# A hybrid encoder block: where attention's low value parts live, and when weights, sums and copies are begun beside it

## The chip, the cores and the metric

The kernel runs on one core of a Trainium2 chip. The metric is the device time of one execution in microseconds, as the median of several runs. PE stands for TensorE's matmul, PEld for its weight loads, DVE for VectorE, ACT for ScalarE, POOL for GpSimd and SP for SyncE, which issues most DMAs here.

## The reference

A stream of 16 learned meta tokens and 1024 tokens of width 1024 goes through one layer. u is the normed input, z = u @ w_in its projection into ten parts. Branch A is a bidirectional retention of four heads in chunks of 128, branch B a windowed attention of eight heads that share two groups of keys and values. The cut below leaves out the norms, gates and padding.

```python
def step(state, kv_c):
    return chunk_decay * state + kv_c, state
...
o_r = _bidirectional_retention(rq, rk, rv, lg_f, lg_b)   # forward scan + backward scan over chunks
y_r = (groupnorm(o_r) * ret_nw * silu(rg)) @ w_rb
...
s = concat(q . k over 3 neighbouring chunks, q . k over the meta keys) * scale
m = max(s, sink);  p = exp(s - m) / (sum(exp(s - m)) + exp(sink - m))
o_a = p @ v                                              # band and meta values
y_a = (o_a * silu(ag)) @ w_ab
mix = sigmoid(gr) * y_r + sigmoid(ga) * y_a
return h + rms_norm(mix @ w_out) * post_w
```

## The kernel before, in words

**Numbers in two parts.** An operand of a matmul is split into a high part (a cast to float32r) and a low part (the operand less its high part), and a product is three matmuls, high by high, low by high and high by low (`mm3`, line 71). So nearly everything that PE reads first passes one cast, on ACT or POOL, and one subtraction on DVE (`dve_lo`, line 88). A weight unit is 256 columns wide; it comes from HBM in two halves of 512 KB each (`fetch_w`, tag `wr`, two buffers) and `split_w` (line 108) makes `wh` on ACT or POOL and `wl` on DVE, both halves one after the other.

**Retention** (`retention`, line 451) runs for four heads. For each head a forward scan over nine chunks (`stage1`, `stage2`) is followed by a backward scan from chunk 8 to 1 (line 585): DVE advances the state `Sb`, POOL and DVE split it, PE forms `pb`, DVE adds it to `op`, takes the group's mean and variance, POOL the power of the variance, DVE normalises `op`, and two chunks later PE transposes it (`to`, line 574), ACT evacuates it to `ost` and SP stores pairs of chunks to `oTr_d`. A filler gives PE other matmuls in between: for heads 0 to 2 the next head's queries and keys, for head 3 the attention keys of group 0, parts of the gate products and the first attention query projection. The rotated queries and keys' sums live in tiles of pool `ra`: tag `q` has six buffers of 512 columns (`qr` of the retention heads, then `aq` of the attention queries, then the softmax rows `p` of even heads).

**Attention.** After retention its pool `rp` is closed and its memory is given to the pools `ap` and, from the other side, `aw` (line 1259). `gen_av` (line 1266) projects the values of the nine chunks: `pav` in one of three PSUM banks `pj`, then its high part `vah` on ACT and its low part `val` on DVE. `vah` lies in a pool that was there before; `val` (line 1263) lies in `ap`. Meta values go to `vm`. Then 32 chunks follow, four pairs of heads (hp) by eight blocks (n), counted here from 0 to 31. `stage1` (line 1287) makes the scores `ps` of both heads in the two PSUM banks `p2`, a masked maximum on DVE (line 1318) into `raw`, the exponential on ACT into `p`, a reciprocal on DVE and the scaling of `p` on POOL. `stage2` (line 1335) transposes `p` on PE into `pt1` and `pt2` (two banks, `p1`), and splits them: `pah` on ACT and `pal` on DVE, `pm` for the meta keys, `pbh` and `pbl` for the third key block. `stage3` (line 1369) multiplies with the values into `po`, ACT evacuates it to `oa` and SP stores it to `oTa_d`.

**The order of the work.** The loop at line 1398 puts, for each chunk k, stage 1 of chunk k+1, stage 2 of k, a number of fill steps (`FILL`, line 26) and stage 3 of k-1. A fill step is three matmuls. The fill is one list of projections (line 1389): attention queries `paq`, keys `pak` of group 1, and parts of the gate products `pe`. Beside it run the hooks (`BEGUN`, line 1425): after fill step n the functions listed under n are recorded. They fetch weights (`fetch_aq`, `fetch_ak`, `pre_fetch`, `sum_fetch`), split them (`parts_aq`, `parts_ak`, `pre_parts`), split queries (`split_q`, line 638: `aqh` on ACT, `aql` on DVE), split keys (`keys`, line 677: `kTh`, `kTl`), and form differences of x (`sum_row`, line 713). `hooked` (line 790) records them behind the last exponential and reciprocal (`marks`); `tc.issue_after` and `follow` tell the scheduler what to put them behind, and it then fixes one order for each engine. `x_to_out` (line 1438) copies 768 of the 1024 rows of x to the output in three DMAs on SP; it is recorded after chunk 13. After attention come the gate, branch and output products (`bz`, `br`, `ba`, `bo`), which are near half of the span.

## Time and profile before

| | |
|---|---|
| median of 3 runs | 1091.0 us (1089.63 to 1092.32) |
| the profiled execution | 1090.71 us |
| its span, first to last instruction | 1088.9 us |
| mean granted TensorE clock | 0.993 |
| ACT, POOL busy | 47%, 19% |
| DMA | 175.17 MB, 161 GB/s on the mean |

The span is what the trace shows; the execution's time has 1.8 us more around it. Retention ends near 340 us, attention runs from there to about 590 us, and the rest are the gate, branch and output products. Matmuls are pipelined: a row of PE lasts longer than the distance to the next one, so work is counted by the distance of rows and lost time by what a stretch took beyond that. A row's last bracket gives the idle time before it on its engine and what ended it.

### The profile page before, as it was taken

The page shows a single profiled execution, that of the slowest core. Times are in us where ns is not written, and L with a number is a line of the kernel's source. Part 1 is how long each engine was busy: PE and PEld are TensorE (multiplying, and loading weights), DVE is VectorE, ACT ScalarE, POOL GpSimd, SP SyncE. Part 2 cuts the span into 40 slices and gives each one's busy share as a digit, 9 for nine tenths or more (in the row PEclk, how much of TensorE's full clock was granted, in tenths as well). Part 3 has the DMA queues.
Part 4 walks back from the last instruction along what each step waited for, and adds up shares of the span by engine and source line. Part 5 has one row for each costly group of instructions (what it writes and reads, how often), then busy time and mean ns, then how long its engine had stood idle before and what let it go on. Part 6 is the DMA issues. An engine that isn't in the chain of part 4 may idle for free.

```text
span 1088.9 us, 17108 instructions
## 1 busy us (share of the span) xinstructions
PE 1060.2 (97%) x5939; PEld 914.8 (84%) x5939; DVE 878.6 (81%) x1789; ACT 510.1 (47%) x1118; POOL 209.8 (19%) x268
## 2 busy tenths in 40 slices
PE   8999999999998999998999999999999999999997
PEld 6898999988988888887888888887888888787886
DVE  7897778878975777877867999999889889867765
ACT  7241432512513556655567654545556546433442
POOL 3234225233332222322320000000000000010032
PEclk9999999999998999999999999999999999999999
DMA  7121102113121152452357678899944656779463
GB/s 289 39 69 58 47 34 69 58 49 98 50 78 39 45 173 94 155 194 88 126 170 263 245 259 286 268 363 331 376 175 139 221 201 199 230 203 324 137 116 78
DMA packets 82902, 175.17 MB, mean 161 GB/s; under 512 B 8784, under 2 KB 22608, under 8 KB 82000
## 3 DMA queue, kind: packets, MB, share of 16 engines
q1 hardware_dynamic: 78928, 167.51, 44.9%
q0 software_dynamic: 3456, 6.29, 3.7%
q8 instruction: 47, 0.77, 0.3%
q14 instruction: 39, 0.32, 0.1%
q10 hardware_dynamic: 432, 0.28, 0.1%
HBM read 119.52 MB, written 57.67 MB: 163 GB/s over the span
## 4 chain that ended last, share of the span: by engine, by line
PE 81%; DVE 9%; DMA 6%; issue 2%; ACT 2%; POOL 0%; SPq 0%; DVEq 0%; POOLq 0%; ACTq 0%
PE bz L73 6%; PE bz L74 6%; PE bz L75 6%; PE pv L73 3%; PE pv L74 2%; PE pv L75 2%; PE br L74 2%; PE br L75 2%; PE br L73 2%; PE bo L74 2%; PE bo L73 2%; PE bo L75 2%; PE ba L74 2%; PE paq L74 2%; PE ba L75 2%
## 5 line engine op out<-in xcount | busy, mean ns | idle before, releaser
L1180 POOL DMA_DIRECT2D mx_d<-c1a x4 | 3.7, 920 | 401.8 <-DVE c1a L1171 401.8
L75 PE MATMUL bz<-T,lhz 128*128 128x512 f32 x192 | 75.8, 395 | 0.0
L74 PE MATMUL bz<-T,llz 128*128 128x512 f32 x192 | 75.8, 395 | 0.0
L73 PE MATMUL bz<-T,lhz 128*128 128x512 f32 x192 | 75.2, 394 | 0.0
L73 PE MATMUL pv<-wh,big 128*128 128x256 f32 x256 | 73.1, 286 | 1.2 <-DVE m_qk L181 1.2
L74 PE MATMUL pv<-wh,big 128*128 128x256 f32 x256 | 73.0, 285 | 0.0
L75 PE MATMUL pv<-wl,big 128*128 128x256 f32 x256 | 72.7, 284 | 0.0
L74 PE MATMUL bz<-big,llz 128*128 128x512 f32 x176 | 69.7, 396 | 0.0
L73 PE MATMUL bz<-big,lhz 128*128 128x512 f32 x176 | 69.1, 396 | 0.4 <-ACT lhz L880 0.3
L75 PE MATMUL bz<-big,lhz 128*128 128x512 f32 x176 | 69.3, 394 | 0.0
L1321 ACT ACTIVATE p<-raw,nm 128x401 f32<-128x401 f32 (+1 forms) x64 | 38.3, 599 | 48.9 <-DVE nm L1318 48.9
L1331 POOL TENSOR_SCALAR p<-p,den 128x400 f32<-128x400 f32 (+1 forms) x60 | 38.7, 659 | 110.6 <-DVE den L1324 109.0
L73 PE MATMUL paq<-big,wh 128*128 128x512 f32 x128 | 51.8, 405 | 0.0
L74 PE MATMUL paq<-big,wl 128*128 128x512 f32 x128 | 50.6, 396 | 0.0
L75 PE MATMUL paq<-big,wh 128*128 128x512 f32 x128 | 50.4, 394 | 0.0
L73 PEld LDWEIGHTS pv<-wh,big 128*128 128x128 f32 x256 | 48.2, 188 | 1.7 <-DVE m_qk L181 1.5
L74 PEld LDWEIGHTS pv<-wh,big 128*128 128x128 f32 x256 | 48.2, 188 | 0.2
L75 PEld LDWEIGHTS pv<-wl,big 128*128 128x128 f32 x256 | 48.3, 189 | 0.0
L1318 DVE CUSTOM_DVE_ANT_0 raw<-ps,mask,nsink 128x400 f32<-128x400 f32 (+1 forms) x64 | 36.1, 597 | 13.8 <-PE ps L75 13.6
L75 PEld LDWEIGHTS bz<-T,lhz 128*128 128x128 f32 x192 | 36.2, 188 | 8.4
L73 PEld LDWEIGHTS bz<-T,lhz 128*128 128x128 f32 x192 | 36.2, 188 | 8.4
L74 PEld LDWEIGHTS bz<-T,llz 128*128 128x128 f32 x192 | 36.2, 188 | 8.4
(630 smaller groups left out, 3624.9 us busy)
## 6 DMA issues: line engine op xcount, KB each, us to landing
wrz<-in_w_in_dram SPq DMA_DIRECT2D x32, 512.0 KB, 5.7
wr<-in_w_in_dram SPq DMA_DIRECT2D x29, 512.0 KB, 3.6
e<-e SPq DMA_DIRECT2D x40, 256.0 KB, 3.7
we<-in_w_in_dram SPq DMA_DIRECT2D x16, 512.0 KB, 3.8
tg<-tg_d SPq DMA_DIRECT2D x32, 256.0 KB, 5.0
T<-preT SPq DMA_DIRECT2D x6, 1024.0 KB, 7.6
oTr_d<-ost SPq DMA_DIRECT2D x16, 256.0 KB, 2.1
xs<-in_xT_dram SPq DMA_DIRECT2D x8, 512.0 KB, 3.8
```

Source lines behind the costliest of these rows:

```text
L73: nc.tensor.matmul(o, ah, bh, start=first, stop=False, **kw)
L74: nc.tensor.matmul(o, al, bh, start=False, stop=False, **kw)
L75: latest[:] = [nc.tensor.matmul(o, ah, bl, start=False, stop=last, **kw).ins]
L1180: nc.gpsimd.dma_start(d, to, accum_op=ALU.add)
L1318: nc.vector.tensor_tensor_reduce(raw[e_][:, 1:1 + wid], s[:, 0:wid], mask[:, mo:mo + wid], -SCALE, nsink[:, hd:hd + 1], ALU.add, ALU.min, ...
L1321: last["exp"] = nc.scalar.activation(p[:, 0:1 + wid], raw[e_][:, 0:1 + wid], AF.Exp, scale=-1.0, bias=nm_[:, e_:e_ + 1], accum_out=den[:, ...
L1331: nc.gpsimd.tensor_scalar(pt[e_][:, 0:wid], pt[e_][:, 0:wid], den[:, e_:e_ + 1], 1.0, op0=ALU.mult, op1=ALU.mult)
```

## The change

Five things change. (1) `val` becomes four tiles of the ring `q` in pool `ra`, two chunks in each, in place of a tile of `ap`; the softmax rows `p` of both heads now come from `ap` with four buffers. (2) The order at the start of attention: the last two value chunks are recorded behind the last transposition of retention (`last["to"]`) and ahead of stage 1 of chunk 0, and chunk 0's fill goes before its stage 2. (3) A weight's two halves are split by two hooks some steps apart (`half_w`), the gate weights' sums are split from their parts (`pre_sums`, `pre_parts`), and `sum_row` comes in two parts; the last lo and hi operations of a chunk join the marks that hooks are recorded behind. (4) `FILL` gives the first two head pairs 114 steps (before 105) and the last two 86 (95), and `BEGUN` has new places for nearly all hooks. (5) `x_to_out` is recorded after chunk 17 in place of 13, and the list of fill has `gen_aq(2, 1)` and `gen_ak(1, (2, 3))` unbroken.

```diff
-FILL = (8, 8, 6, 7, 6, 6, 7, 6), (6, 7, 6, 6, 7, 6, 6, 7), (7, 8, 8, 6, 6, 6, 7, 7), (6, 6, 5, 5, 5, 5, 8)
+FILL = (8, 8, 7, 7, 7, 7, 7, 7), (7,) * 8, (7, 6, 6, 6, 6, 6, 6, 5), (5, 5, 5, 5, 5, 5, 8)
...
-    def split_w(raw, u, act=False):
+    def halves_w(u):
         hi, lo = [], []
-        for s, t in enumerate(raw):
-            h = wp.tile([P, 4, 256], R, tag="wh", bufs=4, name=f"wh{u}_{s}")
-            l = wp.tile([P, 4, 256], R, tag="wl", bufs=4, name=f"wl{u}_{s}")
+
+        def split(t, act):
+            h, l = (wp.tile([P, 4, 256], R, tag=f"w{x}", bufs=4, name=f"w{x}{u}_{len(hi)}") for x in "hl")
             if act:
                 nc.scalar.copy(h, t)
             else:
             dve_lo(l, t, h)
             hi.append(h)
             lo.append(l)
-        return (lambda k, a, b: hi[k // 4][:, k % 4, a:b]), (lambda k, a, b: lo[k // 4][:, k % 4, a:b])
+
+        return split, ((lambda k, a, b: hi[k // 4][:, k % 4, a:b]), (lambda k, a, b: lo[k // 4][:, k % 4, a:b]))
 
     def load_w(src, u, act=False):
-        return split_w(fetch_w(src, u), u, act)
+        split, w = halves_w(u)
+        for t in fetch_w(src, u):
+            split(t, act)
...
+                last["to"] = nc.tensor.transpose(to[:, P * e_:P * e_ + P], o[:, P * e_:P * e_ + P], ident).ins
...
-        wq[hp] = fetch_w(w_in, U_AQ + hp)
-
-    def parts_aq(hp):
-        wq[hp] = split_w(wq[hp], U_AQ + hp, True)
+        raw = fetch_w(w_in, U_AQ + hp)
+        split, wq[hp] = halves_w(U_AQ + hp)
+        begun["q", hp] = lambda s: split(raw[s], True)
+
+    def fetch_ak():
+        raw = fetch_w(w_in, U_AK)
+        split, w_ = halves_w(U_AK)
+        wak.append(w_)
+        begun["k", 1] = lambda s: split(raw[s], True)
+
+    def half_w(which, i, s):
+        begun[which, i](s)
+
+    begun = {}
...
-    def sum_row(k):
+    def sum_row(k, part):
 
         x = {}
         for i, t in xsum.items():
-            nc.scalar.activation(t, t, AF.Copy, scale=vec[:, 4 * i + k:4 * i + k + 1])
+            if not part:
+                nc.scalar.activation(t, t, AF.Copy, scale=vec[:, 4 * i + k:4 * i + k + 1])
             for j in range(2):
                 x[i, j] = t[:, 512 * j:512 * j + 512]
-        for n, o, a, b in SUMS:
+        for n, o, a, b in SUMS[2 * part:2 * part + 2]:
...
-    def pre_parts(u):
+    def pre_sums(u):
 
         g = nc.vector.tensor_tensor
-        raw, n = fetched_w.pop(u), P * len(PRE[u])
+        raw, n = fetched_w[u], P * len(PRE[u])
         t = raw[-1]
         if n > P:
             v = t[:, :, P:n]
             g(v, raw[0][:, :, P:n], v, ALU.add)
             g(v, v, raw[0][:, :, 0:P], ALU.subtract)
             g(v, t[:, :, 0:P], v, ALU.subtract)
+
+    def pre_parts(u):
+
+        t, n = fetched_w.pop(u)[-1], P * len(PRE[u])
...
-                with follow(*marks("exp", "sum")):
+                with follow(*marks("exp", "sum", "lo", "hi")):
...
+    val = [ra.tile([P, 512], R, tag="q", bufs=6, name=f"val{b}") for b in range(NB // 2)]
     pm = [ap.tile([P, 256], R, name=f"pm{i}") for i in range(2)]
-    val = ap.tile([P, NB, 256], R, name="val")
     for t in (vm, pm[0], pm[1]):
         nc.vector.memset(t.bitcast(F32), 0.0)
+    def low_value(b):
+        return val[b // 2][:, 256 * (b % 2):256 * (b % 2) + 256]
...
-                nc.vector.scalar_tensor_tensor(val[:, c - 1], t[:, 0:256], rcol[:, c:c + 1],
+                nc.vector.scalar_tensor_tensor(low_value(c - 1), t[:, 0:256], rcol[:, c:c + 1],
...
-                p = (ap.tile([P, 401], F32, tag="p", bufs=2, name=f"p{hd}_{n}") if e_ else
-                     ra.tile([P, 512], F32, tag="q", bufs=6, name=f"p{hd}_{n}"))
+                p = ap.tile([P, 401], F32, tag="p", bufs=4, name=f"p{hd}_{n}")
...
-                               gen_ak(1, (0, 1)), gen_aq(2, 1, (0,)), gen_ak(1, (2,)), gen_aq(2, 1, (1,)),
-                               gen_ak(1, (3,)), gen_aq(3, 0), gen_aq(3, 1), pre], BEGUN)])[0]
+                               gen_ak(1, (0, 1)), gen_aq(2, 1), gen_ak(1, (2, 3)), gen_aq(3, 0), gen_aq(3, 1), pre], BEGUN)])[0]
         av = gen_av()
         next(av)
+        with follow(last["to"]):
+            next(av, None)
         with follow(*latest):
             stage1(0, 0)
-        with follow(*latest):
-            next(av, None)
         for k, (hp, n) in enumerate(chunks):
             ends = k >= len(chunks) - 2
             if k + 1 < len(chunks):
                 with follow(*latest):
                     fill(FILL[hp][n])
                 yield
+            if not k:
+                with follow(*latest):
+                    fill(FILL[hp][n])
             with follow(*latest, *marks("exp", "sum")) if not ends else ExitStack():
                 stage2(hp, n)
-            if not ends:
+            if k and not ends:
                 with follow(*latest):
                     fill(FILL[hp][n])
             with follow(*latest) if not ends else ExitStack():
                     stage3(*chunks[k - 1])
             if ends:
                 yield
-            if k == 13:
+            if k == 17:
...
-    BEGUN = {0: [(pre_fetch, 7)], 6: [(pre_parts, 7)], 7: [(fetch_aq, 1)], 12: [(split_q, 0, 0, 1)],
-             16: [(parts_aq, 1)], 18: [(sum_fetch, 0)], 20: [(split_q, 0, 1, 1)], 28: [(sum_row, 0)],
-             30: [(pre_fetch, 8)], 36: [(split_q, 1, 0, 0)], 38: [(pre_parts, 8)], 40: [(fetch_aq, 2)],
-             44: [(split_q, 1, 1, 0)], 52: [(split_q, 1, 0, 1)], 56: [(parts_aq, 2)], 58: [(fetch_ak,)],
-             60: [(split_q, 1, 1, 1)], 68: [(parts_ak,)], 70: [(sum_fetch, 1)], 76: [(split_q, 2, 0, 0)],
-             80: [(sum_row, 1)], 84: [(sum_fetch, 2), (split_q, 2, 1, 0)], 94: [(sum_row, 2)], 100: [(keys, 1, 1)],
-             106: [(fetch_aq, 3)], 108: [(split_q, 2, 0, 1)], 116: [(keys, 1, 2)], 120: [(parts_aq, 3)],
-             124: [(sum_fetch, 3), (split_q, 2, 1, 1)], 132: [(keys, 1, 3)], 134: [(sum_row, 3)],
-             138: [(pre_fetch, 9)], 140: [(split_q, 3, 0, 0)], 148: [(pre_parts, 9), (split_q, 3, 1, 0)],
-             150: [(pre_fetch, 10)], 156: [(split_q, 3, 0, 1)], 158: [(pre_parts, 10)], 160: [(pre_fetch, 11)],
-             164: [(split_q, 3, 1, 1)], 170: [(pre_parts, 11)], 172: [(pre_fetch, 12)], 178: [(pre_parts, 12)],
-             180: [(pre_fetch, 13)], 188: [(pre_parts, 13)]}
+    BEGUN = {0: [(pre_fetch, 7)], 4: [(pre_sums, 7)], 6: [(pre_parts, 7)], 8: [(fetch_aq, 1)],
+             12: [(split_q, 0, 0, 1)], 16: [(half_w, 'q', 1, 0)], 19: [(half_w, 'q', 1, 1)],
+             20: [(split_q, 0, 1, 1)], 21: [(sum_fetch, 0)], 30: [(sum_row, 0, 0)], 33: [(sum_row, 0, 1)],
+             34: [(pre_fetch, 8)], 36: [(split_q, 1, 0, 0)], 41: [(pre_sums, 8)], 44: [(split_q, 1, 1, 0)],
+             45: [(pre_parts, 8)], 46: [(fetch_aq, 2)], 52: [(split_q, 1, 0, 1)], 55: [(half_w, 'q', 2, 0)],
+             58: [(half_w, 'q', 2, 1)], 60: [(split_q, 1, 1, 1)], 61: [(fetch_ak,)], 70: [(half_w, 'k', 1, 0)],
+             73: [(half_w, 'k', 1, 1)], 75: [(sum_fetch, 1)], 76: [(split_q, 2, 0, 0)], 82: [(sum_row, 1, 0)],
+             84: [(split_q, 2, 1, 0)], 86: [(sum_row, 1, 1)], 88: [(sum_fetch, 2)], 95: [(sum_row, 2, 0)],
+             98: [(sum_row, 2, 1)], 100: [(keys, 1, 1), (sum_fetch, 3)], 108: [(sum_row, 3, 0), (split_q, 2, 0, 1)],
+             111: [(sum_row, 3, 1)], 113: [(fetch_aq, 3)], 116: [(split_q, 2, 1, 1)], 121: [(half_w, 'q', 3, 0)],
+             122: [(keys, 1, 2)], 125: [(half_w, 'q', 3, 1)], 131: [(keys, 1, 3)], 138: [(pre_fetch, 9)],
+             140: [(split_q, 3, 0, 0)], 145: [(pre_sums, 9)], 148: [(split_q, 3, 1, 0)], 150: [(pre_parts, 9)],
+             151: [(pre_fetch, 10)], 156: [(split_q, 3, 0, 1)], 157: [(pre_sums, 10)], 160: [(pre_parts, 10)],
+             161: [(pre_fetch, 11)], 164: [(split_q, 3, 1, 1)], 167: [(pre_sums, 11)], 169: [(pre_parts, 11)],
+             171: [(pre_fetch, 12)], 175: [(pre_sums, 12)], 177: [(pre_parts, 12)], 179: [(pre_fetch, 13)],
+             184: [(pre_sums, 13)], 187: [(pre_parts, 13)]}
```

Hook 113 fetches the last query weight, hooks 121 and 125 split its halves; `keys(1, i)` splits piece i of the second key group, which the scores of the third and fourth head pair read.

More of the change, by code (lines that the diff above doesn't have):

```diff
@@ L119, in split_w @@
             lo.append(l)
-        return (lambda k, a, b: hi[k // 4][:, k % 4, a:b]), (lambda k, a, b: lo[k // 4][:, k % 4, a:b])
+        return split, ((lambda k, a, b: hi[k // 4][:, k % 4, a:b]), (lambda k, a, b: lo[k // 4][:, k % 4, a:b]))
     def load_w(src, u, act=False):
-        return split_w(fetch_w(src, u), u, act)
+        split, w = halves_w(u)
+        for t in fetch_w(src, u):
+            split(t, act)
+        return w
     big = [[keep.tile([P, 4, T], R, name=f"big{i}_{s}") for i in range(2)] for s in range(2)]
@@ L573, in finish @@
             for e_ in range(2):
-                nc.tensor.transpose(to[:, P * e_:P * e_ + P], o[:, P * e_:P * e_ + P], ident)
+                last["to"] = nc.tensor.transpose(to[:, P * e_:P * e_ + P], o[:, P * e_:P * e_ + P], ident).ins
             if c % 2 == 0:
@@ L667, in block_kernel @@
     wak = []
-    def fetch_ak():
-        wak.append(fetch_w(w_in, U_AK))
-    def parts_ak():
-        wak[0] = split_w(wak[0], U_AK, True)
     rotated_k = {}
@@ L774, in gen_pre @@
             pre_fetch(u)
+            pre_sums(u)
             pre_parts(u)
@@ L1355, in stage2 @@
             nc.scalar.copy(m[0:NM], t2[0:NM, 0:256])
-            nc.scalar.copy(m[64:64 + NM], t2[0:NM, 0:256])
+            last["hi"] = nc.scalar.copy(m[64:64 + NM], t2[0:NM, 0:256]).ins
             last["lo"] = dve_lo(m[32:32 + NM], t2[0:NM, 0:256], m[0:NM])
@@ L1363, in stage2 @@
                 bl_ = ap.tile([P, 256], R, tag="pbl", bufs=2, name=f"pbl{hp}_{n}")
-                nc.scalar.copy(bh_, t2[:, 256:512])
+                last["hi"] = nc.scalar.copy(bh_, t2[:, 256:512]).ins
                 last["lo"] = dve_lo(bl_, t2[:, 256:512], bh_)
@@ L1373, in stage3 @@
             for j, (b, h_, l_) in enumerate(bl):
-                mm3(po[:, 0:256], *(t[:, b, P * g:P * g + P] for t in (vah, val)), h_, l_, j == 0, False)
+                mm3(po[:, 0:256], *(t[:, P * g:P * g + P] for t in (vah[:, b], low_value(b))), h_, l_, j == 0, False)
             latest[:] = [nc.tensor.matmul(po[:, 0:256], vm[0:80, P * g:P * g + P], m[0:80], start=False,
```

## The prediction, made before the change was run

> **What bounds the kernel now.** The page first: part 1 says which engine to count on, and the windows say where it is not full.

> ```profile
> span 1088.9 us, 17108 instructions
> PE 1060.2 (97%) x5939; PEld 914.8 (84%) x5939; DVE 878.6 (81%) x1789; ACT 510.1 (47%) x1118; POOL 209.8 (19%) x268
> ```

> PE is busy 1060.2 of 1088.9 us and the change neither adds nor removes a matmul, so the change is worth the PE holes that it closes less those that it opens. The profiled execution took 1090.71 us, 1.8 more than its span and 0.3 less than the median of the runs, 1091.0; I sum against 1090.71. The holes lie in two places. Windows of 2.5 us (duration, PE, PEld, DVE, ACT, POOL, then granted clock, DMA share, GB/s) show the first, where retention ends and attention begins:

> ```profile
> 332.50:335.00 2.50, 1.98 (x10) 1.51 (x9) 2.17 (x10) 0.63 (x2) 1.23 (x2) 0.65 0.00 0
> 335.00:337.50 2.50, 1.32 (x6) 0.58 (x4) 1.95 (x9) 1.11 (x4) 1.30 (x2) 0.50 0.31 105
> 340.00:342.50 2.50, 2.50 (x13) 2.50 (x13) 0.24 (x3) 0.38 (x1) 0.00 (x0) 0.50 0.32 105
> 342.50:345.00 2.50, 2.50 (x20) 2.50 (x19) 1.65 (x3) 0.48 (x1) 0.00 (x0) 0.80 0.00 0
> ```

> PE has holes, the granted clock falls inside the first of these windows (0.65 is its mean), and it is 0.50 from 340 although PE is full again. The timeline of PE and of DVE there tells why:

> ```profile
> 329.88 0.28 PE L73 MATMUL pb<-Shb,qh 128*128 128x256 f32 x1
> 330.00 0.28 PE L74 MATMUL pb<-Shb,ql 128*128 128x256 f32 x1
> 332.33 0.36 PE L73 MATMUL pb<-Shb,qh 128*128 128x256 f32 x1 [0.67 <-DVE mv L603]
> 334.39 0.41 PE L75 MATMUL pb<-Slb,qh 128*128 128x256 f32 x1
> 338.03 0.66 PE L574 MATMUL to<-ident,op 128*128 128x128 f32 x2 [0.20 <-DVE op L606]
> 338.76 0.58 PE L73 MATMUL pav<-wh,big 128*128 128x256 f32 x1
> 343.58 0.28 PE L74 MATMUL pav<-wh,big 128*128 128x256 f32 x1
> 337.88 0.55 DVE L1265 MEMSET pm<- 128x256 f32 x2
> 338.35 1.14 DVE L1278 SCALAR_TENSOR_TENSOR val<-pav,rcol,vah 128x256 fp32r<-128x256 f32 x3
> 342.26 0.22 DVE L1315 COPY raw<-nsink 128x1 f32<-128x1 f32 x2 [2.77 <-DMA oTr_d<-ost]
> ```

> pav1 to pav3 fill the three pj banks; their val rows run together at 338.35, behind the memset of the pool that takes over retention's memory. Until then pav4 has no bank. From 329.88 to 343.58, 13.7 us, PE does 12 pb and 22 pav matmuls (0.12 apart at full clock, rows 329.88 and 330.00) and six pairs of to (about 0.2 each): 5.3 us of work. **8.4 us are lost there.** The second place is the rest of attention, by the waits of PE from 330 to 590 (rows of the first place left out):

> ```profile
> PE ps L74 <- DVE aql L89: 3.4, 2, 2.4
> PE pt L1344 <- DVE pbl L89: 2.8, 4, 1.0
> PE pt L1341 <- DVE pal L89: 1.3, 1, 1.3
> PE ps L73 <- ACT aqh L642: 0.5, 1, 0.5
> ```

> These 8 waits are 8.0 us; counted from start to start they are about 0.16 longer each (a pb row lasts 0.28 and the next starts after 0.12): **9.3 us**. The longest are at 496:

> ```profile
> 495.32 2.89 DVE L89 TENSOR_TENSOR wl<-wr,wh 128x1024 fp32r<-128x1024 f32 x2
> 498.13 0.68 DVE L89 TENSOR_TENSOR aql<-aq,aqh 128x512 fp32r<-128x512 f32 x1
> 498.86 0.45 PE L74 MATMUL ps<-kTh,aql 128*128 128x400 f32 x1 [2.39 <-DVE aql L89]
> ```

> Both halves of a weight stand in DVE's queue ahead of the query part that the next scores need.

> **The change, part by part.** Prices (mean ns in the middle) are from the groups by shape of 343 to 590:

> ```profile
> L89 DVE TENSOR_TENSOR pal<-pt,pah 128x512 fp32r<-128x512 f32 x32 | 22.1, 689 | 5.9 <-ACT pah L1352 5.8
> L89 DVE TENSOR_TENSOR wl<-wr,wh 128x1024 fp32r<-128x1024 f32 x8 | 10.8, 1382 | 1.3 <-ACT wh L114 1.2
> L181 DVE TENSOR_TENSOR m_aq<-paq,sr 64x512 f32<-64x512 f32 x14 | 9.7, 694 | 0.2
> L114 ACT CAST wh<-wr 128x1024 fp32r<-128x1024 f32 x8 | 8.0, 1046 | 0.1
> L684 ACT CAST kTh<-akr 128x256 fp32r<-128x256 f32 x4 | 1.6, 404 | 0.4 <-POOL akr L182 0.3
> ```

> *val in the q ring.* The ring exists all through retention and its old tiles are read last in the forward scan, so each val may follow its pav. In the built order of the changed program pav4 to pav6 (72 matmuls, 8.5 us) stand between the pb of the last backward scan. What stays open: (a) the last step. Between the last pb (334.39) and the last to (338.03) lie 3.64 us of DVE and POOL steps; a val (0.48) joins them, full clock saves about 0.7 of it, and pb's slot and two pairs of to fill some 0.9; about 2.4 us idle. (b) The order is now pav7, pav8, ps of chunks 0 and 1. The raw copies wait for a DMA of retention until 342.26, 4.2 us after the last to, and the two aql behind them take 1.4, 5.6 together; 48 pav matmuls are 5.7 and hide that, just; without them it would cost as much. But four ps now share two p2 banks, and the second pair waits for the mask operations of the first: 0.7. (c) Chunk 0's fill goes before its stage 2, so three rope rows (2.1) stand before pal (0.69) on DVE: 2.95 with start-up, while PE has 6 transposes and 6 ps (1.74) before it needs pal's bank: 1.2. Together 4.3 in place of 8.4: **-4.1**.

> *Halves, sums and key parts behind lo and hi.* Of the 9.3 us I go through the built DVE order. Stays: the first query weight, whose halves (hooks 16 and 19) still stand both before the aql of hook 20, 1.2; aql behind sums and rope before chunk 8, 0.7; pbl behind three xs sums (as large as a pal: 2.1) and a rope (2.1) after chunk 14, 1.0. The other waits up to 490 go, their operations being behind the chunk's parts now. **-9.3 + 2.9 = -6.4**, if nothing comes in place of the wait at 496.

> *The copies of x to the output move from chunk 13 to 17.* This is what I think comes in its place. On SP the changed order is: last stores of xs, wr17_0, oa of chunk 15, the three copies, **wr17_1**, the second half of the last query weight. SP's rows of before, and the landings counted from issue (SP window by window), show what a transfer behind the copies suffers:

> ```profile
> 456.18 0.67 SPq L1442 DMA_DIRECT2D out_dram<-in_x_dram  x1
> 458.78 0.52 SPq L722 DMA_DIRECT2D xsT<-xs  x1
> xsT<-xs SPq DMA_DIRECT2D x1, 256.0 KB, 11.8
> 463.57 0.33 SPq L710 DMA_DIRECT2D xs<-in_xT_dram  x1
> xs<-in_xT_dram SPq DMA_DIRECT2D x1, 512.0 KB, 8.7
> wr<-in_w_in_dram SPq DMA_DIRECT2D x1, 512.0 KB, 4.3
> ```

> The store issued right behind them landed at 470.6, 14.4 us after the first copy's issue, and a 512 KB load two stores later at 472.3, 16.1 after; a wr load in free queues takes 4.3. So wr17_1 lands some 15 us after the first copy. That copy goes out about 1.5 us after PE ends po of chunk 15 (pah, pm and aqh are before oa on ACT). From that po, call it zero: landing 16.5, wh 1.05, wl 1.38, start-up: 19.0. The spacing of PE's rows, from its timeline, prices what it can do meanwhile:

> ```profile
> 315.05 0.39 PE L75 MATMUL paq<-big,wh 128*128 128x512 f32 x1
> 315.28 0.39 PE L73 MATMUL paq<-big,wh 128*128 128x512 f32 x1
> 489.91 0.60 PE L1341 MATMUL pt<-ident,p 128*128 128x128 f32 x4
> 490.35 0.38 PE L1344 MATMUL pt<-ident,p 128*16 128x128 f32 x2
> 494.80 0.34 PE L73 MATMUL ps<-kTh,aqh 128*128 128x400 f32 x1
> 494.98 0.34 PE L74 MATMUL ps<-kTh,aql 128*128 128x400 f32 x1
> ```

> A paq takes 0.23, a transpose 0.11, a ps 0.18, and po and pak are as wide as pb. In the built order 12 ps (2.2), 16 transposes (1.7), 7 po and 21 pak (3.3) and 13 paq (3.0) come before the first matmul that reads this wl: 10.2. **+8.8.** Inside it lies the wait of the third chunk's ps for keys(1, 2), whose kTh stands on ACT behind wh17_0 and whose kTl on DVE behind wl17_0 (about 3.3), and one of 0.8 for pm, so these aren't added. Bounds: 14.4 with nothing in front of the landing's start gives +8, and 4.1 if the load escapes the queue.

> *The clock.* The granted clock fell at 333 when PE's holes were shorter than 0.7 us each but close together. A hole of 3 us and one of 1.3 will do the same. By the windows above half clock lasted until PE had been full for 3.4 us or more (340 to 343.5), which costs half of that or more: 1.7 to 3.4, **+2**. [...]

> *FILL.* The number of fill steps is 200 before and after; four more come in the first eight chunks, where DVE has room, and hide in the same matmuls. I take 0 (bounds -1 and +1, one longest pbl wait of the rows above).

> Sum: 1090.71 - 4.1 - 6.4 + 8.8 + 2 = **1091.0**: no change that a measurement of this kernel can tell (about 0.3%, 3.3 us).

> **Rivals.** *The load isn't late*: either the queue serves it beside the copies or the built order's margin is larger. Then only 3.3 + 0.8 stay and the clock holds: 1091 - 4.7 - 2 = 1084.3. For it: no row shows a weight load behind such copies; against it: the 8.7 of the other 512 KB load. *The load is later still*: on SP, wr17_0 (512 KB) and two stores are just ahead of the copies, which in before had only 256 KB stores ahead. If the queue takes them strictly one after the other, the landing comes 19 us after the first copy, and PE waits 4 more: 1095. It is slower by 0.3% from a landing 18.3 us after the first copy. *The backward scan isn't filled*: val waits for a ring buffer after all, and the 4.1 stay: 1095.1. Against it: the old ring tiles have no reader in the backward scan. [...]

> **How the numbers follow.** Forecast (1091) 0.40; load not late 0.22; later still 0.20; scan not filled 0.08; clock holds 0.10. The forecast has about 2.5 us to each side (the landing, 14.4 to 16.1; the clock, 1.7 to 3.4; FILL). Faster by over 0.3% is the first rival and a little of the forecast and of the last: 0.27; slower likewise 0.30; within, 0.43. The range takes in both ends of the outer rivals but a tenth on each side: 1084.5 to 1096.

> **What would show it.** Step one is right if PE's row shows pav between the pb, with clock 1.00 to 345 and one hole of about 2.4 us before the last to. Step two: the aql wait at 379 stays, those of pbl near 441 and 462 go. Step three: wr17_1's landing and an ACT row of wh with a DMA as its releaser near 490, and PE holes of 8 to 9 us between the po of chunk 15 and chunk 19. I'm wrong if that wh never waits for a DMA, if the clock falls in the backward scan, or if the z products after 590 have lost or gained more than 1 us, since I give the change nothing there.

## The result, and the profile after

The changed kernel takes **1105.0 us** (median of 4 runs, 1104.1 to 1105.2), the kernel before, on the same chip, 1091.6. The ratio is **1.0124, 95% interval 1.0106 to 1.0141**: 13 us slower. The forecast was 1091.0, with a range to 1096; it was wrong. The profiled execution took 1105.16 us. The page of the changed kernel:

```profile
span 1103.4 us, 17177 instructions
PE 1064.3 (96%) x5939; PEld 917.9 (83%) x5939; DVE 879.3 (80%) x1789; ACT 508.9 (46%) x1118; POOL 202.9 (18%) x268
```

PE does the same 5939 matmuls; its busy time grew by 4.1 us, while the profiled execution took 14.5 us longer. To find the rest, take for each PE row the time to the next row's start, less what that shape usually takes at full clock. This loss, summed by stretch, holds holes and half clock alike:

| stretch, us | before | after | difference |
|---|---|---|---|
| 0 to 320 | 20.0 | 20.1 | +0.1 |
| 320 to 400 | 10.2 | 9.2 | -1.1 |
| 400 to 440 | 1.0 | 7.1 | +6.0 |
| 440 to 480 | 4.2 | 2.6 | -1.6 |
| 480 to 520 | 3.9 | 12.0 | +8.1 |
| 520 to 560 | 1.0 | 0.4 | -0.6 |
| 560 to 580 | 0.2 | 3.8 | +3.6 |
| 580 to the end | 6.3 | 6.0 | -0.3 |
| all | 46.8 | 61.0 | +14.2 |

Three places lose. The waits of PE between 330 and 600 in the changed kernel (total, times, longest) name them:

```profile
PE ps L74 <- DVE aql L89: 4.9, 2, 4.0
PE paq L73 <- ACT wh L114: 3.7, 1, 3.7
PE ps L73 <- ACT kTh L692: 2.5, 1, 2.5
PE to L578 <- DVE op L610: 2.3, 2, 1.9
PE pt L1357 <- DVE pal L89: 2.1, 1, 2.1
PE pt L1360 <- DVE raw L1332: 1.6, 1, 1.6
PE pe L73 <- ACT weh L780: 0.8, 1, 0.8
PE pe L74 <- DVE wel L89: 0.8, 1, 0.8
```

Two windows show what becomes of the clock there, first in the kernel before, then in the changed one (the number ahead of the last two is the granted clock):

```profile
400.00:425.00 25.00, 24.46 (x142) 21.24 (x141) 19.43 (x42) 13.51 (x33) 7.14 (x10) 1.00 0.16 53
500.00:525.00 25.00, 24.60 (x141) 21.33 (x140) 18.57 (x42) 15.15 (x39) 7.88 (x10) 1.00 0.35 124
```

```profile
400.00:425.00 25.00, 20.71 (x104) 17.43 (x103) 18.49 (x37) 9.45 (x24) 5.94 (x8) 0.86 0.43 127
500.00:525.00 25.00, 20.53 (x101) 17.47 (x99) 12.34 (x31) 10.12 (x27) 5.42 (x8) 0.87 0.32 111
```

Before, the longest wait of PE in attention was 2.4 us; now one of 4.0 and one of 3.7 stand there, and in each of the two windows PE started about 40 matmuls fewer than before. The clock was 1.00 in both and is 0.86 and 0.87. Between 300 and 600 it is at half for 20.5 us in five falls (363, 414, 500, 510, 568); before, for 10.2 us in one.

**The place at 412.** The timeline of SP, DVE and PE in the changed kernel:

```profile
402.34 0.38 SPq L731 DMA_DIRECT2D xsT<-xs  x1
406.63 0.33 SPq L761 DMA_DIRECT2D we<-in_w_in_dram  x1
406.78 0.69 DVE L89 TENSOR_TENSOR pal<-pt,pah 128x512 fp32r<-128x512 f32 x1 [0.31 <-ACT pah L1368]
410.39 0.69 DVE L771 TENSOR_TENSOR we<-we,we 128x512 f32<-128x512 f32 x1 [2.93 <-DMA we<-in_w_in_dram]
411.12 0.41 DVE L89 TENSOR_TENSOR pm<-pt,pm 16x256 fp32r<-16x256 f32 x1
414.29 0.42 DVE L89 TENSOR_TENSOR pbl<-pt,pbh 128x256 fp32r<-128x256 f32 x1
416.14 0.68 DVE L89 TENSOR_TENSOR aql<-aq,aqh 128x512 fp32r<-128x512 f32 x1
416.88 0.59 PE L74 MATMUL ps<-kTh,aql 128*128 128x272 f32 x1 [3.98 <-DVE aql L89]
```

Read it from the bottom: PE waits 3.98 us for aql; aql is only the last of a queue. DVE stood still for 2.93 us at the sum of gate weight 8 (L771), whose second load was issued at 406.63. That load takes the buffer of the fourth row sum, whose store went out at 402.34 and had to land first: it landed at 406.57, the load at 410.20. The hooks put that store at step 33, the load at 34 and the sum at 41: seven steps are shorter here than a store of 4.2 us and a load of 3.6.

**The place at 505.** SP, ACT and PE:

```profile
490.69 0.38 SPq L731 DMA_DIRECT2D xsT<-xs  x1
491.60 2.43 SPq L1464 DMA_DIRECT2D out_dram<-in_x_dram  x3
496.33 0.35 SPq L105 DMA_DIRECT2D wr<-in_w_in_dram  x1
507.83 1.04 ACT L114 CAST wh<-wr 128x1024 fp32r<-128x1024 f32 x1 [2.81 <-DMA wr<-in_w_in_dram]
508.93 0.50 PE L73 MATMUL paq<-big,wh 128*128 128x512 f32 x1 [3.71 <-ACT wh L114]
```

The second half of the query weights for heads 6 and 7 is cast 16.2 us after the first copy went out; the forecast had it land after 15 (14.4 to 16.1). But SP issues its load only 4.7 us after that copy, so something else held the load as well: the store of a row sum, issued at 490.69, landed 5.6 us later, at 496.27, and the load went out behind that landing, into the same two buffers.

**The place at 565** was not in the forecast. DVE and PE:

```profile
564.08 0.69 DVE L773 TENSOR_TENSOR we<-we 128x512 f32<-128x512 f32 x1
566.54 1.23 DVE L89 TENSOR_TENSOR wel<-we,weh 128x1024 fp32r<-128x1024 f32 x1 [0.57 <-ACT weh L780]
566.56 0.50 PE L73 MATMUL pe<-big,weh 128*128 128x512 f32 x1 [0.79 <-ACT weh L780]
567.82 0.66 PE L74 MATMUL pe<-big,wel 128*128 128x512 f32 x1 [0.76 <-DVE wel L89]
```

The sums and parts of gate weight 11 now stand behind the chunk's own pal, pm and pbl, and PE's first products with that weight come in the same chunk.

### The profile page after: what moved, and what is told of

Its sections match the earlier page's. It is cut to its first block, busy times and chain, and to the rows that moved or that the text cites. A ratio compares the mean times of both kernels' runs of the same rounds, so it can differ in the third digit from the quotient of the medians.

```text
span 1103.4 us, 17177 instructions
## 1 busy us (share of the span) xinstructions
PE 1064.3 (96%) x5939; PEld 917.9 (83%) x5939; DVE 879.3 (80%) x1789; ACT 508.9 (46%) x1118; POOL 202.9 (18%) x268
## 4 chain that ended last, share of the span: by engine, by line
PE 75%; DVE 11%; DMA 8%; issue 3%; ACT 2%; POOL 1%; SPq 0%; DVEq 0%; POOLq 0%; ACTq 0%
PE bz L73 6%; PE bz L74 6%; PE bz L75 6%; PE pv L73 3%; PE pv L74 2%; PE pv L75 2%; PE br L74 2%; PE br L73 2%; PE br L75 2%; PE bo L74 2%; PE bo L73 2%; PE bo L75 2%; PE ba L74 2%; PE ba L73 2%; PE ba L75 2%
## 5 line engine op out<-in xcount | busy, mean ns | idle before, releaser
L75 PE MATMUL bz<-T,lhz 128*128 128x512 f32 x192 | 75.8, 395 | 0.0
L74 PE MATMUL bz<-T,llz 128*128 128x512 f32 x192 | 75.7, 394 | 0.0
L73 PE MATMUL bz<-T,lhz 128*128 128x512 f32 x192 | 75.2, 394 | 0.0
L73 PE MATMUL pv<-wh,big 128*128 128x256 f32 x256 | 73.2, 286 | 1.2 <-DVE m_qk L185 1.2
L74 PE MATMUL pv<-wh,big 128*128 128x256 f32 x256 | 73.0, 285 | 0.0
L75 PE MATMUL pv<-wl,big 128*128 128x256 f32 x256 | 72.7, 284 | 0.0
L74 PE MATMUL bz<-big,llz 128*128 128x512 f32 x176 | 69.7, 396 | 0.0
L73 PE MATMUL bz<-big,lhz 128*128 128x512 f32 x176 | 69.0, 396 | 0.5 <-ACT lhz L894 0.5
L75 PE MATMUL bz<-big,lhz 128*128 128x512 f32 x176 | 69.3, 394 | 0.0
L1347 POOL TENSOR_SCALAR p<-p,den 128x400 f32<-128x400 f32 (+1 forms) x60 | 35.4, 605 | 118.7 <-DVE den L1340 105.8
L73 PE MATMUL paq<-big,wh 128*128 128x512 f32 x128 | 53.4, 417 | 3.7 <-ACT wh L114 3.7
L74 PE MATMUL paq<-big,wl 128*128 128x512 f32 x128 | 52.2, 408 | 0.8 <-DVE wl L89 0.8
L75 PE MATMUL paq<-big,wh 128*128 128x512 f32 x128 | 51.9, 406 | 0.0
L73 PEld LDWEIGHTS pv<-wh,big 128*128 128x128 f32 x256 | 48.2, 188 | 1.7 <-DVE m_qk L185 1.5
L74 PEld LDWEIGHTS pv<-wh,big 128*128 128x128 f32 x256 | 48.2, 188 | 0.2
L75 PEld LDWEIGHTS pv<-wl,big 128*128 128x128 f32 x256 | 48.3, 189 | 0.0
L74 PEld LDWEIGHTS bz<-T,llz 128*128 128x128 f32 x192 | 36.2, 188 | 8.4
L73 PEld LDWEIGHTS bz<-T,lhz 128*128 128x128 f32 x192 | 36.2, 188 | 8.4
L75 PEld LDWEIGHTS bz<-T,lhz 128*128 128x128 f32 x192 | 36.2, 188 | 8.4
## 6 DMA issues: line engine op xcount, KB each, us to landing
wrz<-in_w_in_dram SPq DMA_DIRECT2D x32, 512.0 KB, 5.8
wr<-in_w_in_dram SPq DMA_DIRECT2D x29, 512.0 KB, 3.7
e<-e SPq DMA_DIRECT2D x40, 256.0 KB, 3.6
we<-in_w_in_dram SPq DMA_DIRECT2D x16, 512.0 KB, 3.6
tg<-tg_d SPq DMA_DIRECT2D x32, 256.0 KB, 5.0
oTr_d<-ost SPq DMA_DIRECT2D x16, 256.0 KB, 2.1
xs<-in_xT_dram SPq DMA_DIRECT2D x8, 512.0 KB, 3.6
```

What stands on the lines that cost most here:

```text
L73: nc.tensor.matmul(o, ah, bh, start=first, stop=False, **kw)
L74: nc.tensor.matmul(o, al, bh, start=False, stop=False, **kw)
L75: latest[:] = [nc.tensor.matmul(o, ah, bl, start=False, stop=last, **kw).ins]
L1347: nc.gpsimd.tensor_scalar(pt[e_][:, 0:wid], pt[e_][:, 0:wid], den[:, e_:e_ + 1], 1.0, op0=ALU.mult, op1=ALU.mult)
```

## The experiments

Theory A: the loss comes from these three places, where a hook or a copy holds an in-order queue (DVE, SP, ACT) for something that isn't there yet, and the clock falls because of the holes. Rivals: (B) the split into halves, the marks and the fill counts cost as such; (C) the lower values in the ring cost; (D) the clock falls whatever the holes are. Where an edit moves hooks, its lines name each hook behind its fill step, in words and not in the kernel's code. All times are set against the kernel before on the same chip, by ratio; its median there was between 1093.0 and 1093.7 us.

### The copies at their old place

```
-            if k == 17:
+            if k == 13:
```

> The changed kernel with one thing undone: the three copies of x to the output are issued behind chunk 13 again, not behind chunk 17. Theory A (the loss lies in three waits that the new places of hooks and copies make, and in the clock falls behind them): the load of the second half of the query weights for heads 6 and 7 no longer stands behind 1 MB copies on SP, so its cast starts before 500 instead of at 507.83, the PE losses at 504.83 (3.87 us), 508.93 and 510.19 go with the half clock of 509.96, and 480 to 520 loses about 5 us in place of 12.0; what the copies cost in their old place, up to 1.5 us between 440 and 480, comes back. 1105 - 7 + 1 = 1099, between 1096 and 1100. Rival B (halves of the weights, the two new marks and the new fill counts are what costs): the second half is late wherever the copies stand, 1103 or more. Rival C (the lower values in the ring cost): no change, 1105.

Measured: 1.0114 (1.0100 to 1.0129), no gain that can be told. Theory A **missed** here; that the half is late wherever the copies stand is what rival B forecast. SP and ACT of this run:

```profile
463.32 1.28 SPq L1464 DMA_DIRECT2D out_dram<-in_x_dram  x2
493.44 5.91 SPq L731 DMA_DIRECT2D xsT<-xs  x3
504.86 0.33 SPq L105 DMA_DIRECT2D wr<-in_w_in_dram  x1
508.43 1.05 ACT L114 CAST wh<-wr 128x1024 fp32r<-128x1024 f32 x1 [2.46 <-DMA wr<-in_w_in_dram]
```

No copy stands ahead of the load any more, and it goes out 8.5 us later than in the changed kernel. The last row sums are stored only from 493 on, and their buffer is the one that the load needs: the store before it landed at 504.80, the load went out at 504.86. So the lateness hands itself down a chain: loads of row sums, their sums, their stores, then the two halves, all through two buffers. The changed kernel put a third round of row sums (row 3) into this chain ahead of the weights; before, row 3 came behind them. Copies at 463 delay the chain's loads (a store issued at 466.91, behind them, landed 11.8 us later, and a load of row 2 went out at 478.71 instead of 468.11), copies at 491 its end.

### Gate weight 8 fetched sooner

```
-30: sum_row 0 part 0, 33: sum_row 0 part 1, 34: pre_fetch 8, 41: pre_sums 8
+27: sum_row 0 part 0, 29: sum_row 0 part 1, 30: pre_fetch 8, 41: pre_sums 8
```

> The changed kernel with three hooks of the fill moved: the first two halves of row sums at steps 27 and 29 (were 30 and 33), the fetch of gate weight 8 at step 30 (was 34). Its sums stay at step 41. Theory A: the load is issued some 5 us sooner than 406.63, lands before DVE comes to the sums, and the wait of 2.93 us at 410.39 goes; with it the PE loss of 4.7 us at 412 and the half clock of 414.39 to 421.21. 400 to 440 loses about 1.5 us instead of 7.1: 1099.5, between 1098 and 1101. Rival D (the clock falls whatever the holes are): the hole goes, a fall between 400 and 440 stays: 1102. Rival B or C: 1104 or more.

Measured: 1.0072 (1.0057 to 1.0088), 5.7 us less than the changed kernel by the ratios. SP and DVE:

```profile
393.79 0.33 SPq L761 DMA_DIRECT2D we<-in_w_in_dram  x1
402.35 1.55 DVE L771 TENSOR_TENSOR we<-we,we 128x512 f32<-128x512 f32 x1
```

The load goes out 12.8 us sooner than in the changed kernel, and DVE's sum has no releaser: it took 1.55 us, for a reason that the row doesn't show, but it didn't wait for the load. 400 to 440 loses 1.6 us instead of 7.1, and no fall stays there: rival D fails at this place.

### The hooks behind the softmax's marks alone

```
-with follow(*marks("exp", "sum", "lo", "hi")):
+with follow(*marks("exp", "sum")):
```

> The changed kernel, but the hooks of the fill wait for the softmax's marks alone as before the change, not for the chunk's own parts too. Theory A: the load of gate weight 8 and the one behind the copies are as late as they were, so the losses at 412 and 505 stay; a hook's work now stands ahead of a chunk's own parts, so the parts of gate weight 11 come about 1 us sooner and the 2 us lost at 565 go, while pal, pbl or aql come later by as much in other chunks: between 1102 and 1108. Rival B (the order of hooks behind the chunk's own parts is what costs): 1095 or less.

Measured: 1.0091 (1.0076 to 1.0106), 3.6 us less than the changed kernel: by the ratio 1101.5, just below theory A's range, far from rival B's. The loss between 560 and 580 falls from 3.75 to 0.15: behind which of a chunk's parts the hook stands is what made gate weight 11 late. The waits of PE show what comes instead:

```profile
PE paq L73 <- ACT wh L114: 5.2, 1, 5.2
PE pt L1360 <- DVE raw L1332: 3.8, 2, 2.8
PE pt L1357 <- POOL p L1347: 2.5, 1, 2.5
```

The load of gate weight 8 still holds DVE (2.73 us, up to 409.89); what waits for it is now a pair of transposes at 415, 2.8 us, not the scores behind aql with 4.0. The 2.5 us, at 489, are a wait that the changed kernel didn't have.

### The lower values in the ring, and nothing else

The kernel before, with this edit, four softmax buffers of their own and the last value chunks ahead of the first scores; chunk 0's fill stays behind its stage 2:

```
-    val = ap.tile([P, NB, 256], R, name="val")
+    val = [ra.tile([P, 512], R, tag="q", bufs=6, name=f"val{b}") for b in range(NB // 2)]
```

> The kernel before the change with the first part of the change alone: the lower values in the ring of the rotated queries, four softmax buffers of their own in place of two and two of the ring, the rest of the values' projection right behind the last transpose of the backward scan and ahead of the first scores. Hooks, marks, halves, fill counts and copies as before. Theory A: the transition near 340 loses some 4 us less, nothing else moves: 1091.6 - 4 = 1087.5, between 1085.5 and 1089. Rival C (the ring makes the values or the softmax wait somewhere): 1091 or more.

Measured: **0.9985** (0.9972 to 0.9997): faster by 1.6 us, not by 4. Rival C fails. The profile says where the rest went: 320 to 360 loses 6.5 us instead of 8.7. The holes there are 2.07 and 0.61 (last transposes), 0.39 and 0.94 us, 4.0 in all, close to the forecast's 4.3 (which had chunk 0's fill ahead of its stage 2); half clock for 3.4 us comes on top. And 440 to 520 loses 10.9 us in this run, 8.1 in the profile of the kernel before: one more fall, at 499, and two waits of transposes at 480.

### The copies behind the whole chain

```
-            if k == 17:
+            if k == 20:
```

> The changed kernel with the three copies of x to the output behind chunk 20, not 17. The run with the copies at their old place showed the second half of the query weights for heads 6 and 7 just as late: there the copies stood ahead of the loads of the row sums, which hand their buffers on to these weights. So the theory is now: the chain of loads that share two buffers (row sums 1, 2 and 3, then the two halves) has no room left, and whoever puts the copies into it, early or late, pays. Behind chunk 20 they stand behind the whole chain: the second half is issued near 496 and lands near 500.5, before the PE needs it at 504.8; 3.87 + 1.03 + 0.36 us and two half clocks between 500 and 515 go, and the half in front, whose load shares the DMA engines with the copies, comes 1 to 2 us sooner, which takes as much off the 2.7 us at 495. 480 to 520 loses 4 to 5 us in place of 12.0: 1105 - 7 = 1098, between 1096 and 1099.5. Rival (the copies have no part, the chain alone is too long): 1103 or more, the loss at 505 stays. Rival (the copies hold up the loads of gate weight 9 in their new place): a new wait of PE near 540.

Measured: 1.0063 (1.0047 to 1.0079), 6.7 us less than the changed kernel.

```profile
495.37 0.33 SPq L105 DMA_DIRECT2D wr<-in_w_in_dram  x1
499.05 1.05 ACT L114 CAST wh<-wr 128x1024 fp32r<-128x1024 f32 x1 [1.43 <-DMA wr<-in_w_in_dram]
```

SP issues the load at nearly the same time as in the changed kernel (496.33), and the cast starts 3.7 us later instead of 11.5: that difference is the copies. PE waits for this weight no more, and no new wait stands near 540, so the rival of the loads of gate weight 9 fails. The 2.7 us at 495 stay; the forecast that they would shrink was wrong.

### Row 3 behind the weights again

```
-100: sum_fetch 3, 108: sum_row 3 part 0, 111: sum_row 3 part 1, 113: fetch_aq 3
+101: fetch_aq 3, 126: sum_fetch 3, 133: sum_row 3 part 0, 135: sum_row 3 part 1
```

> The changed kernel with the fourth row sums behind the query weights for heads 6 and 7 again, as before the change: those weights fetched at step 101, the row fetched at 126, its sums at 133 and 135; the copies of x stay behind chunk 17. Theory (the change put a third round of row sums into the chain of the two shared buffers ahead of these weights, and that makes them late): both halves are issued before 485, ahead of the copies, the casts wait for no DMA, the 2.7 us at 495 and the 5.3 us from 505 on go, with the half clocks of 500 and 510. 480 to 520 loses 2 to 4 us in place of 12.0: 1105 - 9 = 1096, between 1094 and 1098. Rival (the copies alone make it late): as the weights are issued ahead of them the same gain, but the row sums behind the copies then hold DVE near 510, 2 to 4 us of it come back: 1099.

Measured: 1.0048 (1.0032 to 1.0065), 8.3 us less than the changed kernel, with the copies left behind chunk 17.

```profile
476.41 0.37 SPq L105 DMA_DIRECT2D wr<-in_w_in_dram  x1
481.35 0.33 SPq L105 DMA_DIRECT2D wr<-in_w_in_dram  x1
494.20 1.05 ACT L114 CAST wh<-wr 128x1024 fp32r<-128x1024 f32 x1
495.45 1.05 ACT L114 CAST wh<-wr 128x1024 fp32r<-128x1024 f32 x1
489.71 2.58 SPq L1465 DMA_DIRECT2D out_dram<-in_x_dram  x3
```

Both halves are issued ahead of the copies and both casts run without a wait. So the place at 505 needed two things together: a chain too long to get the load out before the copies, and the copies behind which it then stood. Either one undone frees PE; moving the copies into the middle of the chain doesn't.

### Gate weight 11 alone

```
-160: pre_parts 10, 161: pre_fetch 11, 167: pre_sums 11, 169: pre_parts 11
+158: pre_parts 10, 159: pre_fetch 11, 164: pre_sums 11, 167: pre_parts 11
```

with the sums of 10 at 156 and the fetch of 12 at 168.

> The changed kernel with the hooks of gate weight 11 alone moved: its fetch at step 159 (was 161), sums at 164 (167), parts at 167 (169), the parts of weight 10 at 158 and its sums at 156 to let it go. Theory A: the parts are ready before PE comes to that weight's first product, the 2.0 us lost at 565 and the half clock of 568 go: 3.5 us less than the changed kernel, 1101.5, a ratio to the kernel before of 1.008 to 1.010. Rival (the parts only take their place in the queue from others): a wait of pt or po takes over between 545 and 560, 1.011 or more.

Measured: 1.0101 (1.0087 to 1.0115), 2.5 us less than the changed kernel, an interval that theory A's ratio and the rival's share. The profile tells them apart: 560 to 580 loses 0.16 us instead of 3.75, and no other wait came between 540 and 560 (0.18). The profiled execution has two falls that the changed kernel's has not, at 270 and 345, with no edit near them; how much of the gain such falls took from the median can't be told from one profile.

### The three repairs together

> The changed kernel with all of it: row sums 0 and gate weight 8 fetched sooner, row sums 3 behind the query weights, the copies of x behind chunk 20, and the sums and parts of gate weight 11 three steps sooner (its fetch two). If the causes add up: 5 (at 412) + 9 (480 to 520) + 3.5 (565) = 17.5 us less than 1105: 1087.5, between 1085 and 1090, which is 1.5 to 6 us less than the kernel before the change; the waits that stay are those of the last transposes at 340 (2.7 us), of the values' weights at 359 (2.3), of the query parts at 379 (1.1) and of a bank near 470 (1.7). If the clock falls come whatever the holes are, two or three falls of 1.7 to 3.4 us each remain: 1092 to 1094. If new waits take the place of those removed: 1095 or more.

Measured: **1.0006** (0.9993 to 1.0018): 12.9 of the 13.5 us are back, by the ratios, but 1087.5 was not reached; the causes don't add up. The waits of PE show why:

```profile
PE pt L1357 <- DVE pal L89: 2.1, 1, 2.1
PE pt L1360 <- DVE raw L1332: 2.1, 1, 2.1
PE ps L74 <- DVE aql L89: 1.9, 2, 1.0
PE ps L73 <- ACT kTh L692: 1.8, 1, 1.8
PE pt L1360 <- DVE pbl L89: 1.3, 1, 1.3
```

Some of these the changed kernel had already, behind larger ones; that of pbl is new: the parts of gate weight 11, at step 166, had come to stand ahead of a chunk's own pbl.

### Four more hooks

```
+fill of chunk 0 behind its stage 2, as before the change
-82: sum_row 1 part 0, 86: sum_row 1 part 1, 88: sum_fetch 2
+80: sum_row 1 part 0, 84: sum_row 1 part 1, 86: sum_fetch 2
-122: keys(1, 2) (behind the half of the weights of step 121)
+120: keys(1, 2)
-166: pre_parts 11
+167: pre_parts 11
```

> The kernel with all three repairs, and four more hooks moved to where its profile shows a PE wait left: the fill of the first chunk behind its stage 2 again (PE lost 2.27 us at 361 because pal stood behind the parts of gate weight 7 and the rope), row sums 1 at steps 80 and 84 and the fetch of row 2 at 86 (2.25 us at 473: DVE held by a row sum whose load landed late, 1.94 us), the keys of piece 2 at step 120, ahead of the half of the weights (1.96 us at 492, the cast of 1.05 us in front), the parts of gate weight 11 at step 167 instead of 166 (1.47 us at 552). If the theory holds that each of these is an in-order queue held at the wrong place, they give up to 1.3 + 2.2 + 1.9 + 1.4 = 6.8 us, some of which comes back as smaller waits: 4 to 7 us less than the kernel with the three repairs, a ratio to the kernel before of 0.994 to 0.997 in place of 1.0006. If the waits only move on: 0.998 or more. If the clock falls take the gain: two falls or more between 340 and 600 in its profile and 0.998 or more.

Measured: **0.9963** (0.9952 to 0.9975), 4.7 us less than with the three repairs, and faster than the kernel before. The rows of pal and kTh are gone from the waits of PE, that of raw fell to 0.4 and that of pbl to 0.9; that of aql grew from 1.9 to 2.6. One fall is left, at 380. This kernel keeps the change's halves, marks, fill counts and ring, so these alone don't make a kernel slower than the one before: rival B fails as it was put, though what each of them costs or gives by itself wasn't measured. What cost was where the hooks, the copies and the first fill stood.

### One stretch of values and one split

```
-            if c == NB - 2:
+            if c == NB - 1:
                 yield
-16: half_w q1 0, 19: half_w q1 1, 20: split_q(0, 1, 1)
+16: split_q(0, 1, 1), 17: half_w q1 0, 20: half_w q1 1
```

> The kernel with the repairs and the four moved hooks, and two things more. One of the two 24-product stretches of the values' projection that stood behind the last transposes of the backward scan goes ahead of them, where PE lost 2.07 + 0.61 us at 340; and the split of the query parts 0_11 goes ahead of both halves of the weights for heads 2 and 3 (steps 16, 17 and 20), where PE lost 1.90 us at 377. If the theory holds that at each place the engine has work of its own that stands in the wrong order: 2 to 2.7 us and 1.9 us less, with the half clock of 380 gone too, 4 to 6 us in all, a ratio to the kernel before of 0.991 to 0.993 in place of 0.9963. If the transposes' wait is only moved (the stretch is consumed earlier and nothing is left behind the transposes for the first scores): 320 to 360 loses as much as it did, 5.1 us, and the ratio is 0.994 or more.

Measured: **0.9919** (0.9901 to 0.9937): 8.9 us faster than the kernel before, the fastest of all. All waits of PE between 325 and 600:

```profile
PE pt L1357 <- POOL p L1347: 1.8, 4, 0.7
PE ps L73 <- ACT aqh L646: 1.1, 1, 1.1
PE paq L74 <- DVE wl L89: 1.0, 1, 1.0
PE pt L1360 <- DVE pbl L89: 0.9, 2, 0.5
PE ps L74 <- DVE aql L89: 0.8, 1, 0.8
PE pt L1360 <- DVE raw L1332: 0.2, 1, 0.2
```

The wait of the last transposes, 2.3 us in every run above with the ring, is gone, and so is that of aql at 377. The rival, that the wait only moves on, holds in a part: 1.23 us now stand before the first scores (aqh), and this profile has half clock for 6.8 us at 351, so 320 to 360 loses 6.6 us, not less than the 5.1 of the run above. By the ratios it is 4.8 us faster than that run all the same; with a profile of one execution each, which of the two edits gave how much stays open.

## Why the prediction was wrong, step by step

**What bounds the kernel**: right. All of the 14 us are holes of PE and half clock, between 320 and 580, and the products after 590 didn't change by more than 1 us.

**The lower values in the ring, -4.1**: the mechanism was right, the size was not. The holes of the last transposes were 2.07 + 0.61 (forecast 2.4), that of ps 0.39 (0.7). The wait behind pal was 2.31 (1.2): I had put three rope rows ahead of pal, but three sums of gate weight 7 and its wel stand there as well; with the fill behind stage 2 again, 0.94 were left, a wait for p. And a fall came behind it, at 363. So 320 to 400 gave 1.1 us, not 4.1.

**Halves, sums and key parts, -6.4**: here the prediction **failed**, at the term "aql behind sums and rope before chunk 8, 0.7". It measured 4.7 us of holes (0.48 + 4.24), and with the half clock behind them 6.0. I had counted the DVE rows ahead of aql and taken their operand for landed; the row sums' stores, the buffer they hand on and the seven steps between were in the diff, but I had not followed that load through SP. That is 5.7 us of the 13.5 by the run with the earlier fetch. The same step put gate weight 11 at nothing; it cost 2.0 us of holes and 1.7 of half clock: the sums of a gate weight moved behind pbl, and PE's first use of it did not. And the wait after chunk 14, forecast at 1.0, measured 1.76, at 477. Where 2.9 us of holes were to stay in this step, some 10 stood. What came as forecast: aql at 379 waited 1.07 (1.2), and the waits of pbl near 441 and 462 went, though one of 0.45, for POOL's p, stands at 462.

**The copies, +8.8**: the sum came out (0.38 + 2.71 + 0.45 + 3.87 + 1.03 + 0.36 = 8.8 us between 490 and 512), the cause was half of it. 3.5 of it are the piece of keys and pm, which the prediction counted inside the term (3.3 and 0.8) and which the copies don't make: with the copies behind chunk 20, 3.7 stand there. For the other 5.3 I had it that the copies' new place makes the load late; at their old place the load is late as well. The round of row sums that moved ahead of the weights was the other half. The copies went out 1.8 us after the po of chunk 15 (forecast 1.5), but that po ended at 490, so the cast came at 508, not near 490. The load landed 16.2 us after the first copy (15, 14.4 to 16.1), though its buffer had held it for 4.7 of them, which I had not foreseen: that the size came out so near is in part luck.

**The clock, +2**: this term was mis-sized, since it priced one fall. There were five, and twice the time at half clock (20.5 us against 10.2). In the kernel before PE had 13 rows of pav in 2.5 us at half clock (from 340) and 24 at full (from 345), so I estimate half of 20.5, some 10 us, as the most that they can have cost. Two of the five (500 and 510) came with the holes of the copies' term, which I had. Of the 3.41 us ahead of each fall PE was idle for 1.55 to 2.91 (below), so this term goes with the others; that the clock holds, to which I gave 0.10, is excluded.

**FILL, 0**: not measured by itself. The two fastest kernels (0.9963 and 0.9919) use the new counts.

The rivals priced the load behind the copies from both sides, a backward scan that isn't filled and a clock that holds. That a load at another place would be late, and that five places with holes of 2 to 5 us would each bring a fall of its own, was none of them, and the range could not hold it. None of the three signs that I had named for being wrong appeared, either.

## What to carry to other kernels

Follow every load that a moved hook issues or waits for, back through the buffer it takes to the store that frees it, and count the steps in between in time; a queue of operations is only as early as the last operand in it (here 2.93 us that DVE waited for one load became 3.98 us of PE). When several transfers share two buffers, look at the chain as a whole: a transfer put into it is paid wherever it stands, unless it stands behind the chain's end (the copies behind chunk 13 or 17 gave 1.0114 and 1.0124, behind chunk 20 1.0063). And price a hole with the half clock it brings: here holes of 2 to 5 us that brought a fall cost up to another 1.7 to 3.4, an estimate: half of the 3.41 and 6.83 us at half clock.

## What the runs showed of the hardware

Idle time of that size didn't always bring a fall. Of stretches of 3.41 us that lie whole multiples of 3.413 us from a fall, PE was idle for 1.81 us in the one from 339.29 and for 1.59 in the one from 475.83 (changed kernel), for 1.46 in the one from 459.57 and for 1.75 in the one from 497.11 (before), and the clock stayed at 1.00 behind all four. The same wait didn't always bring one either: with pt waiting 2.1 us for pal, the mean clock from 350 to 375 was 0.93 in the changed kernel and in the runs with gate weight 8 sooner and with the copies behind the whole chain, and 1.00 in the run with row 3 late, whose edit is nowhere near. From 550 to 575, with pe waiting 0.8 us for weh, it was 0.93 in the changed kernel and 1.00 in the run with the copies behind the whole chain. That is one reason why single edits here are worth 1 or 2 us more or less than their holes: a fall of 3.41 us can cost half of that, 1.7 us, by the estimate above.
